# A first product by another set of seven block products, with partial results put into PSUM by ScalarE and VectorE

## The chip, the cores and the metric

The kernel runs on one core of a Trainium2 chip. The metric is the device time of one execution in microseconds (us). Times inside the kernel come from the hardware profile of one execution: TensorE is PE, its weight loads are PEld, VectorE is DVE, ScalarE is ACT, GpSimd is POOL and SyncE is SP.

## The reference

```python
batch, m, k, h, n = 16, 512, 768, 3072, 768
y = np.matmul(x, w1) + b1                    # x (16, 512, 768), w1 (768, 3072)
y = 0.5 * y * (1.0 + erf(y / np.sqrt(2.0)))  # GELU
return np.matmul(y, w2).astype(np.float32)   # w2 (3072, 768)
```

Two matrix products stand around a GELU. All inputs are float32 normal random numbers; the kernel multiplies in bf16 and sums in float32. The 16 x 512 = 8192 rows of x are independent of each other.

## The kernel before

**Pairs.** The 8192 rows are cut into pairs of row groups. A pair holds two halves of `w` rows each: w is 384 in pairs 0 to 9 and 256 in pair 10, the last. Both products are done in blocks, two by two, with seven block products in place of eight (Strassen's way): sums of blocks are multiplied, and sums of the seven results give the four blocks wanted. The first product of pair 0 and of the first `PLAIN = 3` positions of pair 1 is done plainly (`plain`), while the sums of w1 blocks are still being made (`make_w1`).

**First product.** H = 3072 is 24 chunks of 128, and K = 768 is 6 chunks. For a position j (0 to 11) the four results are the chunks j and 12 + j of H for the two halves of the rows: c11, c12, c21 and c22, in the code's order. Each of seven block products (M1 to M7) is three matmuls of 128 x 128 weights with a moving operand of w columns (`product1`, line 162). The weights are seven ready-made forms of w1 for that j, 672 KB, which SP loads from `w1f` in DRAM into a ring of seven slots of `w1t` (`load_slot`). The moving operands are blocks of x, transposed, in `xt` (written by DMA transposes that SP issues, `prepare_x`), and sums of such blocks in `xft`, made by VectorE (`sum_x`).

**PSUM banks.** There are eight banks in three pools: `ps_x` (3), `ps_y` (3) and `ps_z` (2). M4, M5 and M7 are summed in one bank (X), M3, M2 and M6 in another (Y), and M1 has the third (Z), see `BANK`. After each product one engine reads the bank (`evacuate`): ScalarE copies M4 into `x1` and M1 into `z` (line 99), VectorE makes `q` (line 106) and subtracts four times into `tt` (line 109). ScalarE then takes the GELU of two results at a time, from `tt` into `g` (lines 170 and 174, 128 x 768).

**Order of the first product.** Every engine runs its instructions in the order of the program (`inorder`). The steps overlap by hand:

```python
for d, m in ((2, "M7"), (1, "M5"), (0, "M4"), (2, "M6"), (1, "M2"), (0, "M3"), (0, "M1")):
    step1(s - d, m)
```

so the products of one j are spread over three steps. M6, the last user of a slot, issues the reload of that slot for seven positions on.

**Second product.** It uses the same seven products over 12 positions j, for each sub-block of 128 rows (three in a wide pair, two in the last): `part2` (line 205, 12 matmuls of 384 columns for each M), `gsum` for the sums of `g` into `st`, `finish2` for the read-out and the output DMA. M4 and M3 use `g` itself and begin early, between the last products of the first product (`early`). At the end of a pair, while `rest(2, ...)` runs, VectorE makes the input sums of the next pair (`xsums`), and the last group of the pair is `rest(2, "M6")`.

**The last pair.** With w = 256 a first-product matmul streams 256 columns; the second product's matmuls keep 384, since their moving operand is a half of w2.

Of the kernel before, what the change touches and what calls it, by code (L numbers as in the profile page):

```python
# [8 lines left out]
FP32 = mybir.dt.float32  # L9
# [3 lines left out]
P = 128  # L13
# [8 lines left out]


WF = {"M3": 0, "M4": 1, "M1": 2, "M5": 3, "M2": 4, "M6": 5, "M7": 6}
XF = {"M3": 0, "M4": 1, "M1": 2, "M6": 3, "M7": 4}
SF = {"M1": 0, "M5": 1, "M2": 2, "M7": 3, "M6": 4}
BANK = {"M1": "Z", "M3": "Y", "M2": "Y", "M6": "Y", "M4": "X", "M5": "X", "M7": "X"}

# [2 lines left out]
def kernel(  # L31
# [8 lines left out]
    nc = tc.nc  # L40
# [108 lines left out]
            dma(nc.sync, out=slot(idx), in_=w1f[(idx + PLAIN) % HP, :, :])  # L149

    def moving1(m, kc, w):
        if m == "M2":
            return xt[:, kc, 0, :w]
        if m == "M5":
            return xt[:, KH + kc, 1, :w]
        return xft[:, XF[m], kc, :w]

    def product1(t, m, p, j, w):
        ps = bank(t, m)
        forms = slot((p - 1) * HP + j - PLAIN).rearrange("p (f kc c) -> p f kc c", f=7, kc=KH)  # L160
        for kc in range(KH):
            inorder(nc.tensor.matmul(  # L162
                out=ps[:, :w], lhsT=forms[:, WF[m], kc, :], rhs=moving1(m, kc, w),
                start=(kc == 0 and m in ("M1", "M3", "M4")), stop=(kc == KH - 1),
                skip_group_check=True))
        tj = tt[:, j % 2]
        c = {"11": tj[:, 0, :w], "12": tj[:, 1, :w], "21": tj[:, 2, :w], "22": tj[:, 3, :w]}
        evacuate(t, m, w, c)
        if m == "M7":
            inorder(nc.scalar.activation(out=g[:, j, :, :w], in_=tj[:, 0:2, :w], func=ACTF.Gelu,  # L170
                                         bias=b1t[:, j:j + 1], scale=1.0))
        if m == "M6":
            load_slot((p - 1) * HP + j - PLAIN + RING)
            inorder(nc.scalar.activation(out=g[:, HP + j, :, :w], in_=tj[:, 2:4, :w], func=ACTF.Gelu,  # L174
                                         bias=b1t[:, HP + j:HP + j + 1], scale=1.0))


    def rows(h, half, i, j0=0, j1=HP):
# [59 lines left out]
            inorder(nc.sync.dma_start_transpose(out=xt[:, :, half, c0:c0 + P], in_=xb[:]))  # L238

    def sum_x(k, w):  # L240
        b11, b12 = xt[:, :KH, 0, :w], xt[:, :KH, 1, :w]
        b21, b22 = xt[:, KH:, 0, :w], xt[:, KH:, 1, :w]
        if k == 0:
            sub(xft[:, XF["M4"], :, :w], b11, b21)
        elif k == 1:
            sub(xft[:, XF["M3"], :, :w], b22, b12)
        elif k == 2:
            add(xft[:, XF["M1"], :, :w], b11, b22)
        elif k == 3:
            add(xft[:, XF["M7"], :, :w], b21, b22)  # L250
        else:
            add(xft[:, XF["M6"], :, :w], b11, b12)


    def load_w2(j, n):
# [33 lines left out]
    def make_w1():  # L289
        nonlocal made  # L290
        j = (made + PLAIN) % HP
        a = raw(j)
        if made < HP - PLAIN:
            area, o = ((ttb, 0), (ttb, 3072), (xftf, 0), (xftf, SLOT))[made % 4]
        else:
            area, o = ((stf, 0), (stf, SLOT), (ttb, 0))[made - HP + PLAIN]
        made += 1
        s = area[:, o:o + SLOT].rearrange("p (f kc c) -> p f kc c", f=7, kc=KH)
        copy("act", s[:, 0:2], a[:, 0:4:3])
        add(s[:, 2], a[:, 0], a[:, 3])  # L300
        add(s[:, 3:5], a[:, 0:4:2], a[:, 1:4:2])
        sub(s[:, 5], a[:, 0], a[:, 2])
        sub(s[:, 6], a[:, 3], a[:, 1])
        dma(nc.sync, out=w1f[j], in_=area[:, o:o + SLOT])

    def plain(hc, half):
# [95 lines left out]
    late_w2 = [lambda k=k, part=part: make_w2(k, part) for part in range(2) for k in range(9, HP)]  # L402


    for p, (r0, w) in enumerate(pairs):
        ns = w // P
        subs = [dict() for _ in range(ns)]
        most = HP - 2
        nxt = pairs[p + 1] if p + 1 < len(pairs) else None

        def early(i, m, a, b):
            part2(subs[i], m, i, a, b)

        def both(i, a, b, close):
            for m in ("M4", "M3"):
                early(i, m, a, b)
                if close:
                    finish2(subs[i], m, r0, w, i)

        def rest(i, m, after=()):  # L420
            part2(subs[i], m, i, 0, HP)
            finish2(subs[i], m, r0, w, i)
            for f in after:
                f()

        def sums(i, *ms):
            return [lambda m=m: gsum(m, i) for m in ms] if i < ns else []

        def xsums(*ks):
            return [lambda k=k: sum_x(k, nxt[1]) for k in ks] if nxt is not None else []  # L430

        forms = [make_w1] if p == 0 else []

        if p == 0:
            for m in ("M1", "M5", "M2"):
                gsum(m, 0)
                late_w2.pop(0)()
            for f in late_w2:
                f()
            for m in ("M7", "M6"):  # L440
                gsum(m, 0)
            for j in range(HP - 1):
                for i in range(ns):
                    early(i, "M3", j, j + 1)
                for i in range(ns):
                    early(i, "M4", j, j + 1)
            both(0, HP - 1, HP, True)
            both(1, HP - 1, HP, True)
        else:
            js = list(range(PLAIN if p == 1 else 0, HP))  # L450
            if p == 1:
                while made < HP:
                    make_w1()
                for j in range(PLAIN):
                    for hc in (j, HP + j):
                        plain(hc, 0)
                        plain(hc, 1)
                load_raw_slots(PLAIN)
                for k in range(5):
                    sum_x(k, w)  # L460
            ts = [dict() for _ in range(HP)]

            def step1(s, m):
                if 0 <= s < len(js):
                    product1(ts[s], m, p, js[s], w)

            for s in range(len(js)):
                for d, m in ((2, "M7"), (1, "M5"), (0, "M4"), (2, "M6"), (1, "M2"), (0, "M3"), (0, "M1")):
                    step1(s - d, m)
            last = len(js) - 1  # L470
            step1(last - 1, "M7")
            step1(last, "M5")
            early(0, "M4", 0, 5)
            step1(last - 1, "M6")
            step1(last, "M2")
            gsum("M1", 0, 0, most)
            early(0, "M4", 5, most)
            early(0, "M3", 0, most)
            step1(last, "M7")
            step1(last, "M6")  # L480
            gsum("M5", 0, 0, most)
            early(1, "M4", 0, most)
            early(1, "M3", 0, most)
            both(0, most, HP, True)
            gsum("M1", 0, most, HP)
            gsum("M5", 0, most, HP)
            for m in ("M2", "M7", "M6"):
                gsum(m, 0)

        if nxt is not None:  # L490
            prepare_x(*nxt)
        nload = 0

        def load_raw_slots(plain_done=0):
            nonlocal nload
            while nload < RING:
                k = (nload + FIRST) % RING
                need = {j for j in range(HP)
                        if j // 3 * 2 * GRP < (k + 1) * SLOT and (j // 3 + 1) * 2 * GRP > k * SLOT}
                have = {(PLAIN + n) % HP for n in range(made)}  # L500
                if not need <= have or any(plain_done <= j < PLAIN for j in need):
                    break
                load_slot(nload)
                nload += 1

        def forms(n):
            if p > 0:
                return []

            def f():  # L510
                make_w1()
                load_raw_slots()
            return [f] * n

        rest(0, "M1")
        rest(0, "M5", sums(1, "M1"))
        rest(0, "M2", sums(1, "M5"))
        if p == 0:
            both(2, HP - 1, HP, True)
        rest(0, "M7", sums(1, "M2") + forms(1))  # L520
        rest(0, "M6", sums(1, "M7", "M6"))
        if p > 0:
            both(1, most, HP, True)
        rest(1, "M1", forms(1))
        rest(1, "M5", sums(2, "M1") + forms(1))
        rest(1, "M2", sums(2, "M5"))
        rest(1, "M7", sums(2, "M2"))
        rest(1, "M6", sums(2, "M7", "M6"))
        if ns > 2:
            if p > 0:  # L530
                both(2, 0, HP, True)
            later = p == 0
            rest(2, "M1", forms(1) if later else xsums(0, 1))
            rest(2, "M5", forms(1) if later else xsums(2))
            rest(2, "M2", forms(1) if later else xsums(3))
            rest(2, "M7", () if later else xsums(4))
            rest(2, "M6")


# [28 lines left out]
```

## Time and profile before

| what | value |
|---|---|
| runs | 900.15, 900.21 and 901.23 us, median 900.21 |
| span of the profiled execution | 897.6 us |
| its own device time | not listed apart; the median is 2.6 us over the span |
| PE busy | 889.9 us, 5627 matmuls |
| DVE busy | 597.1 us, 1088 instructions |
| ACT busy | 380.4 us, 609 instructions |
| mean granted TensorE clock | 1.000 |
| first product, line 162 | 2457 matmuls, from 111.9 to 869.4 us |

In timeline rows the columns are the start in us, the time the row covers, the engine, the line of the kernel, the operation, what it writes and reads, the shape and the number of instructions merged; in brackets stands how long the engine had been idle, and what released it. In rows of groups, behind the bar stand the busy time in us and the mean duration of one in ns, then the idle time before them. In rows of waits stand the total in us, the number of times and the longest. The recorded duration of a matmul covers its way through the array, so successive matmuls overlap in the record, and their starts tell the rate.

### The profile page before, as it was taken

The numbers are of one execution on the slowest core, as the hardware profiler recorded it, in microseconds if no ns is written. First come the engines' busy times: TensorE is split into PE (matmuls) and PEld (weight loads), VectorE is DVE, ScalarE is ACT, GpSimd is POOL, SyncE is SP. The second block draws the span as 40 slices with busy tenths as digits, with TensorE's granted clock in tenths as the row PEclk, the third lists the DMA queues.
The fourth block names the chain that finished last, engine by engine and source line by source line (L and its number), as shares of the span: only waits on it lengthen the run. The fifth ranks groups of instructions, "written<-read, shape, count | busy, mean of one in ns | idle before, by whom it ended". The sixth has DMA issues, their size and how long they took to land.

```text
span 897.6 us, 14279 instructions
## 1 busy us (share of the span) xinstructions
PE 889.9 (99%) x5627; PEld 544.2 (61%) x5627; DVE 597.1 (67%) x1088; ACT 380.4 (42%) x609; POOL 81.3 (9%) x148
## 2 busy tenths in 40 slices
PE   8999999999999999999999999999999999999998
PEld 5656666666666666666666666666666666666774
DVE  1287776677667676766776676767667766766665
ACT  3542474057217603730571175037306711750460
POOL 6200100100110010001001100100010011001000
PEclk9999999999999999999999999999999999999999
DMA  9997976556736663665557366746645663663411
GB/s 170 206 230 201 377 258 163 122 154 207 162 95 200 197 144 100 205 167 115 175 192 165 94 194 203 141 112 197 167 106 178 205 155 98 194 194 106 146 45 71
DMA packets 89159, 148.30 MB, mean 165 GB/s; under 512 B 50796, under 2 KB 68228, under 8 KB 89092
## 3 DMA queue, kind: packets, MB, share of 16 engines
q1 hardware_dynamic: 65588, 101.77, 37.6%
q0 software_dynamic: 23504, 45.62, 23.0%
q8 instruction: 44, 0.72, 0.3%
q14 instruction: 23, 0.19, 0.1%
HBM read 124.56 MB, written 33.42 MB: 176 GB/s over the span
## 4 chain that ended last, share of the span: by engine, by line
PE 98%; DMA 1%; POOL 0%; issue 0%; ACT 0%; DVE 0%; POOLq 0%
PE psx L205 21%; PE psy L205 21%; PE psx L162 18%; PE psy L162 18%; PE psz L205 7%; PE psz L162 6%; PE psy L312 3%; PE psx L312 3%; DMA st<-in_x_dram 1%; PE psy L375 0%; PE psx L375 0%; PE psz L341 0%; POOL st L74 0%; POOL w1t L74 0%; ACT g L314 0%
## 5 line engine op out<-in xcount | busy, mean ns | idle before, releaser
L162 PEld LDWEIGHTS <-w1t 128*128 128x128 bf16 x2457 | 240.0, 98 | 146.1
L205 PEld LDWEIGHTS <-st 128*128 128x128 bf16 x1920 | 187.6, 98 | 124.4
L99 ACT COPY x<-psx 128x384 f32<-128x384 f32 (+1 forms) x149 | 68.0, 457 | 266.8 <-PE psx L205 191.0
L162 PE MATMUL psx<-xft,w1t 128*128 128x384 bf16 (+1 forms) x702 | 148.6, 321 | 0.0
L162 PE MATMUL psy<-xft,w1t 128*128 128x384 bf16 (+1 forms) x702 | 148.5, 321 | 0.0
L170 ACT ACTIVATE g<-tt,b1t 128x768 bf16<-128x768 f32 (+1 forms) x117 | 106.9, 914 | 86.6 <-DVE tt L109 86.6
L205 PE MATMUL psx<-w2t,st 128*128 128x384 bf16 x768 | 135.3, 326 | 0.0
L205 PE MATMUL psy<-w2t,st 128*128 128x384 bf16 x768 | 135.3, 326 | 0.0
L106 DVE TENSOR_TENSOR q<-x,psy 128x384 f32<-128x384 f32 (+1 forms) x149 | 80.9, 543 | 55.6 <-ACT x L99 40.5
L174 ACT ACTIVATE g<-tt,b1t 128x768 bf16<-128x768 f32 (+1 forms) x117 | 106.7, 912 | 22.6 <-DVE tt L109 22.6
L99 ACT COPY z<-psz 128x384 f32<-128x384 f32 (+1 forms) x149 | 69.8, 468 | 93.6 <-PE psz L205 71.5
L205 PEld LDWEIGHTS <-g 128*128 128x128 bf16 x768 | 75.0, 98 | 50.0 <-issue 0.6
L109 DVE TENSOR_TENSOR tt<-z,psx 128x384 f32<-128x384 f32 (+1 forms) x117 | 63.3, 541 | 51.7 <-PE psx L162 51.7
L109 DVE TENSOR_TENSOR tt<-z,psy 128x384 f32<-128x384 f32 (+1 forms) x117 | 63.3, 541 | 45.9 <-PE psy L162 45.9
L106 DVE TENSOR_TENSOR st<-g 128x1536 bf16<-128x1536 bf16 (+2 forms) x116 | 92.5, 812 | 0.0
L74 POOL DMA_DIRECT2D xb<-in_x_dram x58 | 31.2, 542 | 523.9 <-DMA xt<-xb 515.5
L162 PE MATMUL psy<-xt,w1t 128*128 128x384 bf16 (+1 forms) x351 | 74.3, 321 | 0.0
L162 PE MATMUL psz<-xft,w1t 128*128 128x384 bf16 (+1 forms) x351 | 74.3, 321 | 0.0
L162 PE MATMUL psx<-xt,w1t 128*128 128x384 bf16 (+1 forms) x351 | 74.3, 321 | 0.0
L205 PE MATMUL psx<-w2t,g 128*128 128x384 bf16 x384 | 74.2, 326 | 0.0
L205 PE MATMUL psy<-w2t,g 128*128 128x384 bf16 x384 | 72.9, 326 | 0.3 <-ACT g L314 0.3
L205 PE MATMUL psz<-w2t,st 128*128 128x384 bf16 x384 | 67.7, 326 | 0.0
(53 smaller groups left out, 548.0 us busy)
## 6 DMA issues: line engine op xcount, KB each, us to landing
w1t<-w1f SPq DMA_DIRECT2D x117, 672.0 KB, 4.0
out_dram<-ot POOLq DMA_DIRECT2D x60, 384.0 KB, 2.6
xb<-in_x_dram POOLq DMA_DIRECT2D x58, 192.0 KB, 4.1
w2t<-in_w_dram POOLq DMA_DIRECT2D x8, 576.0 KB, 22.5
w1t<-in_w_dram POOLq DMA_DIRECT2D x7, 576.0 KB, 17.9
w1f<-tt SPq DMA_DIRECT2D x6, 672.0 KB, 4.8
w1f<-xft SPq DMA_DIRECT2D x4, 672.0 KB, 3.6
out_dram<-ot SPq DMA_DIRECT2D x4, 384.0 KB, 2.3
```

What stands on the lines that cost most here:

```text
L74: inorder(queue.dma_start(out=out, in_=in_))
L99: inorder(nc.scalar.copy(out=dst, in_=src))
L106: inorder(nc.vector.tensor_tensor(out=dst, in0=a, in1=b, op=ALU.add))
L109: inorder(nc.vector.tensor_tensor(out=dst, in0=a, in1=b, op=ALU.subtract))
L162: inorder(nc.tensor.matmul(out=ps[:, :w], lhsT=forms[:, WF[m], kc, :], rhs=moving1(m, kc, w), start=(kc == 0 and m in ("M1", "M3", "M4")), ...
L170: inorder(nc.scalar.activation(out=g[:, j, :, :w], in_=tj[:, 0:2, :w], func=ACTF.Gelu, bias=b1t[:, j:j + 1], scale=1.0))
L174: inorder(nc.scalar.activation(out=g[:, HP + j, :, :w], in_=tj[:, 2:4, :w], func=ACTF.Gelu, bias=b1t[:, HP + j:HP + j + 1], scale=1.0))
L205: inorder(nc.tensor.matmul(out=ps[:, :NB], lhsT=lhs, rhs=w2t[:, j, WF[m], :], start=(j == 0 and m in ("M1", "M3", "M4")), stop=(j == HP - ...
L312: inorder(nc.tensor.matmul(out=py[:, :HW], lhsT=lhs[:, kc, (j % 3) * P:(j % 3 + 1) * P], rhs=xt[:, kc, half, :], start=(kc == 0), stop=(kc ...
```

## The change

The first product uses another set of seven products, P1 to P7, and other block sums. They are gathered in three banks for each j:

- c12's bank (pool Z): P1 opens it and P4 adds to it. The GELU reads it from PSUM.
- c11's bank (pool X): ScalarE copies P1 from c12's bank into it, as a start value. P2, P6 and P3 add to it, none of them opening the bank. The GELU reads it from PSUM after P3.
- c22's bank (pool Y): P7 opens it, and VectorE copies it to SBUF (`v`). After P2 VectorE writes c11's bank minus `v` over it, and P5 adds to that. The GELU reads it from PSUM, with scale -1.
- c21 never has a bank: after P6 VectorE writes c11's bank minus `v` to `tt`, and the GELU reads it there, with scale -1.

So VectorE has three instructions for each j where it had five, and ScalarE has one copy and four GELUs of w columns, where it had two copies and two GELUs of 2 w. Four sums of x blocks are made where there were five; the fourth uses the third, which uses the second. The products of one j span two steps. The first two products of a pair, P1 and P7 of its first j, are issued ahead of the last group of the pair before (`ahead`), and in pair 1 ahead of the last plain half.

```diff
-XF = {"M3": 0, "M4": 1, "M1": 2, "M6": 3, "M7": 4}
+W1F = {"P7": 0, "P1": 1, "P2": 2, "P3": 3, "P4": 4, "P6": 5, "P5": 6}
+XF = {"P1": 0, "P3": 1, "P2": 2, "P7": 3}
+XRAW = {"P4": (1, 0), "P6": (0, 1), "P5": (1, 1)}
...
+    def gelu1(j, h, half, src, w, sign):
+        hc = h * HP + j
+        inorder(nc.scalar.activation(out=g[:, hc, half, :w], in_=src, func=ACTF.Gelu,
+                                     bias=b1t[:, hc:hc + 1], scale=sign))
+
     def product1(t, m, p, j, w):
-        ps = bank(t, m)
+        if m == "P1":
+            t["c12"] = ps_z.tile([P, 512], FP32, name="psz")
+            ps = t["c12"]
+        elif m == "P4":
+            ps = t["c12"]
+        elif m == "P7":
+            t["c22"] = ps_y.tile([P, 512], FP32, name="psy")
+            ps = t["c22"]
+        elif m == "P5":
+            ps = t["c22"]
+        else:
+            ps = t["c11"]
...
-                out=ps[:, :w], lhsT=forms[:, WF[m], kc, :], rhs=moving1(m, kc, w),
-                start=(kc == 0 and m in ("M1", "M3", "M4")), stop=(kc == KH - 1),
+                out=ps[:, :w], lhsT=forms[:, W1F[m], kc, :], rhs=moving1(m, kc, w),
+                start=(kc == 0 and m in ("P1", "P7")), stop=(kc == KH - 1),
...
+        if m == "P1":
+            t["c11"] = ps_x.tile([P, 512], FP32, name="psx")
+            copy("act", t["c11"][:, :w], ps)
+        elif m == "P7":
+            t["v"] = evp.tile([P, HW], FP32, name="z")
+            copy("dve", t["v"][:, :w], ps)
+        elif m == "P2":
+            sub(t["c22"][:, :w], ps, t["v"][:, :w])
+        elif m == "P6":
+            sub(tt[:, j % 2, 0, :w], ps, t["v"][:, :w])
+        elif m == "P4":
+            gelu1(j, 1, 0, ps, w, 1.0)
+        elif m == "P3":
             load_slot((p - 1) * HP + j - PLAIN + RING)
+            gelu1(j, 0, 0, ps, w, 1.0)
+        elif m == "P5":
+            gelu1(j, 0, 1, tt[:, j % 2, 0, :w], w, -1.0)
+            gelu1(j, 1, 1, ps, w, -1.0)
...
+        a11, a12 = xt[:, :KH, 0, :w], xt[:, KH:, 0, :w]
+        a21, a22 = xt[:, :KH, 1, :w], xt[:, KH:, 1, :w]
...
+            sub(f[:, XF["P1"]], a11, a12)
+            add(f[:, XF["P3"]], a11, a21)
+            sub(f[:, XF["P2"]], a12, f[:, XF["P3"]])
+            add(f[:, XF["P7"]], f[:, XF["P2"]], a22)
...
+    def ahead(p):
+        j = PLAIN if p == 1 else 0
+        for m in ("P1", "P7"):
+            product1(ts[p][j], m, p, j, pairs[p][1])
...
-                for d, m in ((2, "M7"), (1, "M5"), (0, "M4"), (2, "M6"), (1, "M2"), (0, "M3"), (0, "M1")):
+                if s == 0:
+                    order = ((0, "P2"), (0, "P4"), (-1, "P1"), (0, "P6"))
+                elif s == 1:
+                    order = ((0, "P7"), (1, "P5"), (0, "P2"), (1, "P3"), (0, "P4"), (0, "P6"))
+                else:
+                    order = ((0, "P1"), (0, "P7"), (1, "P5"), (0, "P2"), (1, "P3"), (0, "P4"), (0, "P6"))
+                for d, m in order:
                     step1(s - d, m)
...
-            step1(last - 1, "M7")
-            step1(last, "M5")
+            step1(last, "P5")
             early(0, "M4", 0, 5)
-            step1(last - 1, "M6")
-            step1(last, "M2")
+            step1(last, "P3")
             gsum("M1", 0, 0, most)
             early(0, "M4", 5, most)
             early(0, "M3", 0, most)
-            step1(last, "M7")
-            step1(last, "M6")
...
-            rest(2, "M7", () if later else xsums(4))
+            rest(2, "M7")
+            if nxt is not None and p > 0:
+                ahead(p + 1)
             rest(2, "M6")
```

More of the change, by code (lines that the diff above doesn't have):

```diff
@@ L151, in moving1 @@
     def moving1(m, kc, w):
[L152 to L155, printed above, removed]
+        if m in XRAW:
+            kh, half = XRAW[m]
+            return xt[:, kh * KH + kc, half, :w]
         return xft[:, XF[m], kc, :w]
+    def gelu1(j, h, half, src, w, sign):
+        hc = h * HP + j
+        inorder(nc.scalar.activation(out=g[:, hc, half, :w], in_=src, func=ACTF.Gelu,
+                                     bias=b1t[:, hc:hc + 1], scale=sign))
     def product1(t, m, p, j, w):
-        ps = bank(t, m)
+        if m == "P1":
[10 more added lines that the diff above has]
+            ps = t["c11"]
         forms = slot((p - 1) * HP + j - PLAIN).rearrange("p (f kc c) -> p f kc c", f=7, kc=KH)
@@ L162, in product1 @@
             inorder(nc.tensor.matmul(
-                out=ps[:, :w], lhsT=forms[:, WF[m], kc, :], rhs=moving1(m, kc, w),
-                start=(kc == 0 and m in ("M1", "M3", "M4")), stop=(kc == KH - 1),
+                out=ps[:, :w], lhsT=forms[:, W1F[m], kc, :], rhs=moving1(m, kc, w),
+                start=(kc == 0 and m in ("P1", "P7")), stop=(kc == KH - 1),
                 skip_group_check=True))
[L166 to L172, printed above, removed]
+        ps = ps[:, :w]
+        if m == "P1":
[11 more added lines that the diff above has]
+        elif m == "P3":
             load_slot((p - 1) * HP + j - PLAIN + RING)
-            inorder(nc.scalar.activation(out=g[:, HP + j, :, :w], in_=tj[:, 2:4, :w], func=ACTF.Gelu,
-                                         bias=b1t[:, HP + j:HP + j + 1], scale=1.0))
+            gelu1(j, 0, 0, ps, w, 1.0)
+        elif m == "P5":
+            gelu1(j, 0, 1, tt[:, j % 2, 0, :w], w, -1.0)
+            gelu1(j, 1, 1, ps, w, -1.0)
     def rows(h, half, i, j0=0, j1=HP):
@@ L240, in sum_x @@
     def sum_x(k, w):
-        b11, b12 = xt[:, :KH, 0, :w], xt[:, :KH, 1, :w]
-        b21, b22 = xt[:, KH:, 0, :w], xt[:, KH:, 1, :w]
+        a11, a12 = xt[:, :KH, 0, :w], xt[:, KH:, 0, :w]
+        a21, a22 = xt[:, :KH, 1, :w], xt[:, KH:, 1, :w]
+        f = xft[:, :, :, :w]
         if k == 0:
-            sub(xft[:, XF["M4"], :, :w], b11, b21)
+            sub(f[:, XF["P1"]], a11, a12)
         elif k == 1:
-            sub(xft[:, XF["M3"], :, :w], b22, b12)
+            add(f[:, XF["P3"]], a11, a21)
         elif k == 2:
-            add(xft[:, XF["M1"], :, :w], b11, b22)
-        elif k == 3:
-            add(xft[:, XF["M7"], :, :w], b21, b22)
+            sub(f[:, XF["P2"]], a12, f[:, XF["P3"]])
         else:
-            add(xft[:, XF["M6"], :, :w], b11, b12)
+            add(f[:, XF["P7"]], f[:, XF["P2"]], a22)
     def load_w2(j, n):
@@ L298, in make_w1 @@
         s = area[:, o:o + SLOT].rearrange("p (f kc c) -> p f kc c", f=7, kc=KH)
-        copy("act", s[:, 0:2], a[:, 0:4:3])
-        add(s[:, 2], a[:, 0], a[:, 3])
+        copy("act", s[:, 0:2], a[:, 1:3])
+        add(s[:, 2], a[:, 1], a[:, 2])
         add(s[:, 3:5], a[:, 0:4:2], a[:, 1:4:2])
-        sub(s[:, 5], a[:, 0], a[:, 2])
-        sub(s[:, 6], a[:, 3], a[:, 1])
+        sub(s[:, 5], a[:, 2], a[:, 0])
+        sub(s[:, 6], a[:, 1], a[:, 3])
         dma(nc.sync, out=w1f[j], in_=area[:, o:o + SLOT])
@@ L402 @@
     late_w2 = [lambda k=k, part=part: make_w2(k, part) for part in range(2) for k in range(9, HP)]
+    ts = [[dict() for _ in range(HP)] for _ in pairs]
+    def ahead(p):
+        j = PLAIN if p == 1 else 0
+        for m in ("P1", "P7"):
+            product1(ts[p][j], m, p, j, pairs[p][1])
     for p, (r0, w) in enumerate(pairs):
@@ L450 @@
             js = list(range(PLAIN if p == 1 else 0, HP))
+            last = len(js) - 1
             if p == 1:
@@ L453 @@
                     make_w1()
[L454 to L457, printed above, removed]
+                for k in range(4):
+                    sum_x(k, w)
+                hcs = [hc for j in range(PLAIN) for hc in (j, HP + j)]
+                for hc in hcs:
+                    plain(hc, 0)
+                    if hc == hcs[-1]:
+                        ahead(p)
+                    plain(hc, 1)
                 load_raw_slots(PLAIN)
-                for k in range(5):
-                    sum_x(k, w)
-            ts = [dict() for _ in range(HP)]
             def step1(s, m):
-                if 0 <= s < len(js):
-                    product1(ts[s], m, p, js[s], w)
-            for s in range(len(js)):
-                for d, m in ((2, "M7"), (1, "M5"), (0, "M4"), (2, "M6"), (1, "M2"), (0, "M3"), (0, "M1")):
+                if 0 <= s <= last:
+                    product1(ts[p][js[s]], m, p, js[s], w)
+            for s in range(last + 1):
+                if s == 0:
[5 more added lines that the diff above has]
+                for d, m in order:
                     step1(s - d, m)
-            last = len(js) - 1
-            step1(last - 1, "M7")
-            step1(last, "M5")
+            step1(last, "P5")
             early(0, "M4", 0, 5)
-            step1(last - 1, "M6")
-            step1(last, "M2")
+            step1(last, "P3")
             gsum("M1", 0, 0, most)
```

## The prediction

> **What bounds the kernel now.** I read the page first, then who waited for whom, then the timeline of one step of the first product, once in a wide pair (moving width 384) and once in the last pair (width 256), and last the groups with shapes kept apart.
>
> The page says that TensorE is never without work, at full clock:
>
> ```profile
> span 897.6 us, 14279 instructions
> PE 889.9 (99%) x5627; PEld 544.2 (61%) x5627; DVE 597.1 (67%) x1088; ACT 380.4 (42%) x609; POOL 81.3 (9%) x148
> PEclk9999999999999999999999999999999999999999
> ```
>
> Busy time alone proves little, because the ends of matmuls are modelled. The timeline settles it. These rows are one step of the first product in a wide pair:
>
> ```profile
> 207.97 0.65 PE L162 MATMUL psx<-xft,w1t 128*128 128x384 bf16 x3
> 208.45 0.65 PE L162 MATMUL psx<-xt,w1t 128*128 128x384 bf16 x3
> 208.65 0.56 DVE L109 TENSOR_TENSOR tt<-z,psx 128x384 f32<-128x384 f32 x1 [0.35 <-PE psx L162]
> ...
> 211.38 0.65 PE L162 MATMUL psx<-xft,w1t 128*128 128x384 bf16 x3
> ```
>
> From M7 of one step (207.97) to M7 of the next (211.38) are 3.41 us for 21 matmuls, 0.1625 us each. Twelve matmuls of the second product of the same width take 1.95 us in the chain of waits, again 0.1625 each. In the last pair a step takes 845.99 - 843.70 = 2.29 us, 0.109 us a matmul:
>
> ```profile
> 843.70 0.49 PE L162 MATMUL psx<-xft,w1t 128*128 128x256 bf16 x3
> ...
> 844.23 0.42 DVE L109 TENSOR_TENSOR tt<-z,psx 128x256 f32<-128x256 f32 x1 [0.16 <-PE psx L162]
> ...
> 845.99 0.49 PE L162 MATMUL psx<-xft,w1t 128*128 128x256 bf16 x3
> ```
>
> So rate and count of the matmuls set the time, and in the list of waits TensorE is held by another compute engine once after the start:
>
> ```profile
> PE psy L205 <- ACT g L314: 0.3, 1, 0.3
> ```
>
> That wait lies at 59 us, in pair 0, which the change leaves alone. The first product has nothing to win back; it can only lose.
>
> **The change, part by part.**
>
> *Matmuls.* Seven products of three matmuls before, seven of three after, same widths: 2205 of 384 columns and 252 of 256. Cost 0.
>
> *Work of VectorE and ScalarE.* Per j VectorE loses five additions or subtractions (0.555 us each) and gains one copy and two subtractions. ScalarE trades two copies and two wide GELUs for one copy (0.47) and four GELUs of 384 (the row L314 has 0.58, and they start 0.46 apart when queued, as at 104.72 and 105.18): 0.47 + 4 x 0.46 = 2.3 us of each 3.41. Neither engine bounds anything; relieving them is worth nothing while TensorE has the chain.
>
> *The new waits of TensorE.* Before, every read-out had most of a step before its bank or result was wanted. Now two read-outs stand between products of the same step. The order is P1 P7 P5' P2 P3' P4 P6 (a prime marks the step before).
>
> First wait: P2 waits for ScalarE's copy of P1 into the bank c11. P2 is due three products after P1 begins, 9 x 0.1625 = 1.463 us. A read-out begins 0.69 us after its product begins (207.97 to 208.65, rounded). An instruction whose TensorE wait stands in a wait of its own ahead of it begins about 0.07 later: in the last pair M7's subtraction normally begins 0.53 after M7 (843.70, 844.23), and where it has such a double wait 0.60 after (868.89, 869.49):
>
> ```profile
> 868.89 0.49 PE L162 MATMUL psx<-xft,w1t 128*128 128x256 bf16 x3
> ...
> 869.49 0.42 DVE L109 TENSOR_TENSOR tt<-z,psx 128x256 f32<-128x256 f32 x1 [1.61 <-PE psx L162]
> ```
>
> The new copy has a double wait too; ScalarE's rows of that kind come 0.06 late (a copy at 873.38 begins 0.42 after its last matmul, others 0.36). The copy takes 0.47. From its end to the matmul I take 0.05, from the one stall that the trace shows (58.98 + 0.58 = 59.56, matmul at 59.61):
>
> ```profile
> 58.98 0.58 ACT L314 ACTIVATE g<-psy,b1t 128x384 bf16<-128x384 f32 x1 [0.17 <-PE psy L312]
> 59.61 0.32 PE L205 MATMUL psy<-w2t,g 128*128 128x384 bf16 x1 [0.34 <-ACT g L314]
> ```
>
> Sum: 0.69 + 0.06 + 0.47 + 0.05 = 1.27 of 1.46: hidden with 0.19 to spare. ScalarE must be free then: its last GELU before it (P4' of the step before) begins at five products plus 0.69 = 3.13 and lets go at 3.59, against 3.41 + 0.75 = 4.16. Behind the waiting copy stand the four GELUs, which nobody on TensorE wants within the step.
>
> Second wait: P6 waits until VectorE has read c11 (`sub(t["c22"]...)`, PSUM to PSUM). P6 too is due 9 matmuls after P2 begins. Sum: 0.69 + 0.07 + 0.555 + 0.05 = 1.365 of 1.463: hidden with 0.10 to spare. VectorE is free: its copy of P7 ends by 0.27 after P2 begins. Behind the subtraction waits only P6's own.
>
> In the last pair the same two sums have nine matmuls of 0.1092 = 0.983 us. ScalarE: 0.53 + 0.06 + 0.355 + 0.05 = 0.995, late by 0.01. VectorE: 0.60 + 0.42 + 0.05 = 1.07, late by 0.09. Durations are from
>
> ```profile
> L109 DVE TENSOR_TENSOR tt<-psx,q 128x256 f32<-128x256 f32 x12 | 5.0, 418 | 0.2 <-PE psx L162 0.2
> L99 ACT COPY x<-psx 128x256 f32<-128x256 f32 x12 | 4.3, 355 | 7.9 <-PE psx L162 7.9
> ```
>
> Twelve steps: 12 x 0.09 + 11 x 0.01 = 1.2 us, all on the path.
>
> *The unknown price* is a VectorE or ScalarE write to PSUM; every such row of before writes SBUF. The tail behind an instruction's last read is what could differ: VectorE starts its next 0.46 after one of 0.555 (89.01 to 89.47), a tail of 0.095. With no tail nothing is late anywhere: 0 us, and below nothing it can't go, since TensorE has no idle time there to give. With a tail twice as long the wide pairs still just fit (0.69 + 0.07 + 0.65 + 0.05 = 1.46) and the last pair is late by 0.18 x 12 = 2.2 us. I take the SBUF duration, the nearest row: on the reading side the space makes no difference (fp32 from PSUM: 558 ns for 384 columns and 424 for 256, so 1.05 a column and 156 fixed; bf16 from SBUF: 948 for 1536 and 352 for 384, 0.52 a column and 153 fixed).
>
> The Trainium skill (Perfetto Trace Analysis, section Optimizing Scalar/DVE Operations) gives about 60 ns of access overhead for VectorE on SBUF and 125 on PSUM, and 93 and 51 for ScalarE. On reads the rows here do not agree; on writes no run so far shows it. By it the last pair would be late by 0.155 instead of 0.09 a step, +1.9 us in all.
>
> *Edits at nothing.* The ring reload (`load_slot`) is issued by P3, one step behind, instead of M6, two behind: six products, 2.9 us, earlier on SP; its loads land in 4.0 us, seven steps ahead, and no TensorE wait names them; the x transposes stand behind it as before. P1 and P7 ahead of the second product's last group: P7 needs the fourth input sum, which VectorE makes right after M2's read-out, about 0.36 + 0.56 + 0.75 = 1.7 us after M2's last matmul begins, against 12 + 3 matmuls = 2.4. In pair 1 the five sums end at 108.2 us, and P1 would begin one plain half before 111.93, at 110.95. If one of these covers went, it would cost under 1 us per pair, 10 us in all. One bank of c11, c12 and c22 is reused after 3, 2 and 3 steps, longer than the read-outs take.
>
> **The rivals.**
>
> *VectorE's write to PSUM is longer than 0.655 us in wide pairs (slower).* From there on P6 is late in all 117 steps. At 0.70: 105 x 0.045 + 12 x 0.23 = 7.5 us, 907.7. Between 0.605 and 0.655 only the last pair pays, 1.8 to 2.4 us, 902.0 to 902.6. For it: 0.10 is a thin cover, and no row has this write. Against: VectorE's rows move by less than 10 ns with the source. Chance 0.27 for both together. (The Trainium skill, same section, says that profiled latency is about twice its figures; its difference counted twice makes 0.685 and, as an estimate, 906.)
>
> *No stall at all.* The PSUM write is acknowledged faster, and the last pair just fits: 900.2. Chance 0.08.
>
> *ScalarE becomes late.* Its queue is strict; were the copy delayed by a GELU by more than 0.19, each of 117 steps would pay the rest. Per 0.05 that is 5.9 us, 906. Against: 0.57 us between its last GELU and the copy. Chance 0.06.
>
> *The clock falls.* Should the short stalls of the last pair halve the clock there, its 27.5 us of first product double: about 928. Against: the granted clock is 1.000 in every slice past a 0.5 us stall at 59 us. The Trainium skill (TensorE: Matmul & The Clock Gate, section A second HAM failure mode: psum-queue depth-cycling) reports such a case. Chance 0.03.
>
> *Faster.* It would need time that TensorE loses now; that is some 7 us at the start, which no edit touches, and the 0.3. Chance 0.03, for what I have overlooked.
>
> **How the numbers follow.** The profiled span is 897.6 and the median of the runs 900.21; the 2.6 around the span stay. The forecast is 900.21 + 1.2 = 901.4, with a chance of 0.53 that it ends within 900.4 to 902.0. A measurement of this kernel can tell some 0.2%, 1.8 us, from no change: so forecast and "no stall" count as the same (0.61), the write, ScalarE and the clock as slower (0.36), the rest as faster (0.03). The range runs from 899.9 (no stall, with the runs' scatter) to 904.0, which takes in both ends of the unknown write and the milder half of the slow rival.
>
> **What would show it.** Right: in wide pairs first-product matmuls still 0.1625 apart, P6 without idle time before it; in the last pair about 0.09 before each P6. Wrong: P6 waiting in all pairs (VectorE's write over 0.655), P2 waiting for ScalarE's copy, or TensorE waiting for sums or slots at a pair's start. A time below 898.4 would contradict the bound itself.

## The result and the profile after

| kernel | runs, us | ratio to before, 95% interval |
|---|---|---|
| before | 899.78 to 901.39, median 900.64 (6) | |
| changed | 901.76 to 904.30, median 903.03 (6) | 1.0033, 1.0019 to 1.0047 |

The changed kernel is slower, by 2.4 us in this comparison. It was forecast at 901.4, within 899.9 to 904.0: the median lies in that range, but outside the narrower 900.4 to 902.0, to which the prediction gave a chance of 0.53. A second comparison further down gives 1.0009 (0.9998 to 1.0019), and there the change's part is told from the start's.

The page of after, against that of before: the same matmuls, a fifth less VectorE time (479.8 us in place of 597.1), a span 2.4 us longer, and the granted clock of TensorE full in every slice.

```profile
span 900.0 us, 14009 instructions
PE 890.6 (99%) x5627; PEld 544.6 (61%) x5627; DVE 479.8 (53%) x844; ACT 371.1 (41%) x726; POOL 81.4 (9%) x148
```

VectorE lost 117 us of work and ScalarE 9, and none of it came out as time, since the first product's matmuls had not waited for either before.

A wide step, from the timeline:

```profile
202.71 0.65 PE L179 MATMUL psx<-xft,w1t 128*128 128x384 bf16 x3
202.97 0.57 DVE L111 TENSOR_TENSOR psy<-psx,z 128x384 f32<-128x384 f32 x1 [0.47 <-PE psx L179]
203.20 0.65 PE L179 MATMUL psz<-xt,w1t 128*128 128x384 bf16 x3
203.69 0.65 PE L179 MATMUL psx<-xt,w1t 128*128 128x384 bf16 x3
204.17 0.65 PE L179 MATMUL psz<-xft,w1t 128*128 128x384 bf16 x3
204.66 0.65 PE L179 MATMUL psy<-xft,w1t 128*128 128x384 bf16 x3
204.92 0.46 ACT L101 COPY psx<-psz 128x384 f32<-128x384 f32 x1 [0.45 <-PE psz L179]
205.15 0.65 PE L179 MATMUL psy<-xt,w1t 128*128 128x384 bf16 x3
205.63 1.14 PE L179 MATMUL psx<-xft,w1t 128*128 128x384 bf16 x6
```

The rows are P3', P4, P6, P1, P7, P5' and P2 with P3' again. They begin 0.49 us apart, without a gap: VectorE's subtraction ends at 202.97 + 0.567 = 203.54 and P6 is due at 203.69; ScalarE's copy ends at 205.38 and P2 is due at 205.63.

The same in the last pair:

```profile
850.52 0.43 DVE L111 TENSOR_TENSOR psy<-psx,z 128x256 f32<-128x256 f32 x1 [0.29 <-PE psx L179]
850.59 0.49 PE L179 MATMUL psz<-xt,w1t 128*128 128x256 bf16 x3
851.01 0.49 PE L179 MATMUL psx<-xt,w1t 128*128 128x256 bf16 x3
```

From P4 (850.59) to P6 (851.01) are 0.42 us where three matmuls take 0.33: a wait of 0.09. The subtraction ends at 850.957, P6 begins at 851.01. By the starts of all matmuls, P6 waits 0.09 nine times, 0.03 twice and 0.17 once in the last pair, 1.04 us together.

Two more waits of 0.25 us lie in wide pairs, at 128 and 609 us. The first:

```profile
127.87 0.65 PE L179 MATMUL psz<-xt,w1t 128*128 128x384 bf16 x3
128.00 0.57 DVE L111 TENSOR_TENSOR psy<-psx,z 128x384 f32<-128x384 f32 x1 [0.83 <-ACT g L161]
128.61 0.65 PE L179 MATMUL psx<-xt,w1t 128*128 128x384 bf16 x3
```

Here VectorE's subtraction for P6 began 0.13 after P4, where in the usual step it begins 0.23 ahead of P4 (202.97 against 203.20): 0.36 late, which is more than the cover of 0.10. The ScalarE instruction named in brackets had ended at 127.67.

All waits of the first product add up to 1.54 us, by the starts of successive matmuls less 0.1625 or 0.1092 each; the same sum over before is 0.00. The other 0.8 us of the longer span lies at the start, which the change leaves alone: the first matmuls that need w1 begin at 9.38 in the profile of before and at 10.10 here, both after a wait for the load, and 0.1 more goes into the wait for the next load of w1.

```profile
9.38 1.18 PE L375 MATMUL psx<-xt,w1t 128*128 128x128 bf16 x18 [1.84 <-DMA w1t<-in_w_dram]
```

```profile
10.10 1.18 PE L400 MATMUL psx<-xt,w1t 128*128 128x128 bf16 x18 [3.21 <-DMA w1t<-in_w_dram]
```

### The profile page after: what moved, and what is told of

Its sections match the earlier page's. It is cut to its first block, busy times and chain, and to the rows that moved or that the text cites. A ratio compares the mean times of both kernels' runs of the same rounds, so it can differ in the third digit from the quotient of the medians.

```text
span 900.0 us, 14009 instructions
## 1 busy us (share of the span) xinstructions
PE 890.6 (99%) x5627; PEld 544.6 (61%) x5627; DVE 479.8 (53%) x844; ACT 371.1 (41%) x726; POOL 81.4 (9%) x148
## 4 chain that ended last, share of the span: by engine, by line
PE 98%; DMA 1%; ACT 0%; POOL 0%; issue 0%; DVE 0%; ACTq 0%; POOLq 0%
PE psx L231 21%; PE psy L231 21%; PE psx L179 18%; PE psz L179 12%; PE psy L179 12%; PE psz L231 7%; PE psy L337 3%; PE psx L337 3%; DMA st<-in_x_dram 1%; PE psy L400 0%; ACT g L161 0%; PE psx L400 0%; PE psz L366 0%; DVE psy L111 0%; POOL st L76 0%
## 5 line engine op out<-in xcount | busy, mean ns | idle before, releaser
L179 PE MATMUL psx<-xft,w1t 128*128 128x384 bf16 (+1 forms) x702 | 131.0, 320 | 0.0
L111 DVE TENSOR_TENSOR tt<-psx,z 128x384 f32<-128x384 f32 (+1 forms) x117 | 63.6, 544 | 103.0 <-PE psx L179 103.0
L101 ACT COPY psx<-psz 128x384 f32<-128x384 f32 (+1 forms) x117 | 53.0, 453 | 94.4 <-PE psz L179 94.4
L111 DVE TENSOR_TENSOR psy<-psx,z 128x384 f32<-128x384 f32 (+1 forms) x117 | 64.7, 553 | 49.3 <-PE psx L179 47.6
L103 DVE COPY z<-psy 128x384 f32<-128x384 f32 (+1 forms) x117 | 63.7, 544 | 39.3 <-PE psy L179 39.2
L161 ACT ACTIVATE g<-psx,b1t 128x384 bf16<-128x384 f32 (+1 forms) x117 | 66.6, 569 | 38.5 <-PE psx L179 37.0
L161 ACT ACTIVATE g<-psz,b1t 128x384 bf16<-128x384 f32 (+1 forms) x117 | 66.5, 569 | 26.6 <-PE psz L179 26.6
L161 ACT ACTIVATE g<-tt,b1t 128x384 bf16<-128x384 f32 (+1 forms) x117 | 70.9, 606 | 11.5 <-DVE tt L111 11.5
L179 PE MATMUL psz<-xt,w1t 128*128 128x384 bf16 (+1 forms) x351 | 74.2, 321 | 0.0
L179 PE MATMUL psy<-xft,w1t 128*128 128x384 bf16 (+1 forms) x351 | 74.2, 321 | 0.0
```

The costliest lines, as they stand in the source:

```text
L101: inorder(nc.scalar.copy(out=dst, in_=src))
L103: inorder(nc.vector.tensor_copy(out=dst, in_=src))
L111: inorder(nc.vector.tensor_tensor(out=dst, in0=a, in1=b, op=ALU.subtract))
L161: inorder(nc.scalar.activation(out=g[:, hc, half, :w], in_=src, func=ACTF.Gelu, bias=b1t[:, hc:hc + 1], scale=sign))
L179: inorder(nc.tensor.matmul(out=ps[:, :w], lhsT=forms[:, W1F[m], kc, :], rhs=moving1(m, kc, w), start=(kc == 0 and m in ("P1", "P7")), stop ...
```

## The experiments

**Theory A:** the change costs what its two new waits cost, 1.5 us in the first product; the rest is scatter of the start. **Theory B:** it also lowers the clock, or the loss lies elsewhere.

**1. Before against itself, and the change again.** No edit.

> The kernel before against itself. Theory A (the change costs what TensorE waits for in the first product, 1.5 us in the trace, and the rest of the measured 2.4 us is scatter of the start): ratio 1.000, and the granted clock of the single executions scatters as it does for the changed kernel (0.996 to 1.000). Theory B (the change also lowers the clock in most executions): all executions of this kernel at a clock of 1.000, while the changed kernel has 0.996 to 0.998.

> The changed kernel once more, on the chip of the other runs of this set. Theory A: 1.5 us over before, ratio 1.0017, with 0.09 us of waiting ahead of nine or ten P6 of the last pair and one or two longer waits elsewhere. Theory B: 2.4 us or more, ratio 1.0027 to 1.004, with a clock below that of before.

Measured: before against itself 0.9998 (0.9989 to 1.0007), 901.4 against 901.48 for the 29 executions of before in this set; the change 902.67, ratio 1.0009 (0.9998 to 1.0019). Both kernels have executions at mean clocks from 0.996 to 1.000, so theory B's clock is refuted. Sorted by that clock (means, with the number of executions; the changed kernel has none at 0.997), the difference is much the same in each group, though some groups are small and the times within one differ by up to 2 us:

| mean clock | before against itself | the 29 of before | changed | changed less the 29 |
|---|---|---|---|---|
| 0.996 | 902.07 (1) | 902.32 (11) | 903.48 (1) | 1.16 |
| 0.998 | 901.37 (4) | 901.43 (9) | 902.79 (8) | 1.36 |
| 1.000 | 899.75 (2) | 899.95 (5) | 901.02 (3) | 1.07 |

The trace of the second run of the change has 1.51 us of waits in the first product (1.54 in the first run), ahead of the same instructions. So the change's own cost is 1.1 to 1.4 us by the times and 1.5 by the trace, and of the 2.4 in the first comparison about one is scatter. The scatter's place is in the trace of this run: after the wait for w1 its clock falls for some microseconds.

```profile
8.00:12.00 4.00, 2.07 (x22) 2.08 (x23) 0.00 (x0) 0.00 (x0) 1.67 (x2) 0.78 1.15 199
12.00:16.00 4.00, 3.99 (x59) 3.83 (x57) 1.11 (x2) 1.54 (x3) 3.17 (x4) 0.80 1.27 202
```

These are rows of busy time by stretch; the third number from the end is the granted clock, 1.00 in both stretches in the profiles of before. Here 0.22 and 0.20 of 4 us are missing, 1.7 us at full clock, about as much as lies between the executions of before at 1.000 and at 0.998 (1.5).

**2. P6 later.**

```diff
-    order = ((0, "P1"), (0, "P7"), (1, "P5"), (0, "P2"), (1, "P3"), (0, "P4"), (0, "P6"))
+    order = ((0, "P1"), (1, "P6"), (0, "P7"), (1, "P5"), (0, "P2"), (1, "P3"), (0, "P4"))
```

with the first two steps and the end of a pair to match; there two groups of the second product's early matmuls move too. Between P1 and P2 lie three products then, P6', P7 and P5', not the four that the expectation names.

> P6 of a step is put behind P1 of the next, so that three products instead of two lie between P2 and P6, and four between P1 and P2; nothing else changes. Theory A (P6 waits for VectorE's subtraction into PSUM): P6 is then due 12 x 0.109 = 1.31 us after P2 in the last pair, against a need of 1.07, and 1.95 against 1.36 in the wide pairs, so no matmul of the first product waits: 1.5 us less than the changed kernel, ratio to before 1.000. Theory B (the loss is the clock's or lies outside the first product): the waits go from the trace, but the time stays 1 us or more over before.

Measured: 901.42, ratio 1.0000 (0.9991 to 1.0009). The sum of waits in the first product is 0.00 us again. In the last pair:

```profile
849.01 0.43 DVE L111 TENSOR_TENSOR psy<-psx,z 128x256 f32<-128x256 f32 x1 [0.21 <-ACT g L161]
849.08 0.49 PE L179 MATMUL psz<-xt,w1t 128*128 128x256 bf16 x3
849.41 0.49 PE L179 MATMUL psz<-xft,w1t 128*128 128x256 bf16 x3
849.73 0.49 PE L179 MATMUL psx<-xt,w1t 128*128 128x256 bf16 x3
```

P4, the next P1 and P6 follow each other at 0.33 us; the subtraction ends at 849.44, 0.29 before P6. Theory A holds, and this order takes the change's whole cost away. It does not beat the kernel before: neither has a gap in TensorE's first product.

**3. One product between P2 and P6 instead of two.**

```diff
-    order = ((0, "P1"), (0, "P7"), (1, "P5"), (0, "P2"), (1, "P3"), (0, "P4"), (0, "P6"))
+    order = ((0, "P1"), (0, "P7"), (1, "P5"), (0, "P4"), (0, "P2"), (1, "P3"), (0, "P6"))
```

> From the third step of a pair on, P4 is issued ahead of P2, so that only one product (P3 of the step before) lies between P2 and P6. The sum of the read-out chain (0.69 + 0.06 + 0.57 + 0.05 = 1.37 us wide, 0.59 + 0.43 + 0.05 = 1.07 in the last pair) against six matmuls (0.975 and 0.655) gives a wait of 0.39 us ahead of P6 in 87 wide steps and 0.42 in 10 narrow ones: 34 + 4 us, some 37 us over the changed kernel, near 939. If the chain were not what holds P6 (a rival: the bank is free as soon as VectorE has read its last element, some 0.1 us before the subtraction's recorded end), the wait would be 0.29, and the time near 929.

Measured: 939.57, ratio 1.0424 (1.0398 to 1.0451). By the starts P6 waits 0.388 us in a usual wide step; all waits make 38.0 us, 36.5 over the changed kernel. So the recorded end of the subtraction counts, not an earlier release of the bank, with which P6 would have waited 0.29.

```profile
202.38 0.57 DVE L111 TENSOR_TENSOR psy<-psx,z 128x384 f32<-128x384 f32 x1 [0.96 <-PE psx L179]
203.00 0.65 PE L179 MATMUL psx<-xt,w1t 128*128 128x384 bf16 x3 [0.22 <-DVE psy L111]
```

The row of P6 shows idle time of only 0.22, since the recorded ends of the matmuls ahead are modelled and reach into the wait. The list of waits has the same shortfall:

```profile
PE psx L179 <- DVE psy L111: 22.2, 97, 0.6
```

22 us in place of 38. In the changed kernel, where the waits are 0.03 to 0.25, the list names no such wait at all.

**4. One product between P1 and P2.**

```diff
-    order = ((0, "P1"), (0, "P7"), (1, "P5"), (0, "P2"), (1, "P3"), (0, "P4"), (0, "P6"))
+    order = ((0, "P1"), (0, "P7"), (0, "P2"), (1, "P5"), (1, "P3"), (0, "P4"), (0, "P6"))
```

> From the third step of a pair on, P2 is issued ahead of P5 of the step before: only P7 lies between P1 and P2, and three products between P2 and P6. Theory A (the copy of P1 by ScalarE is a chain of 0.69 + 0.06 + 0.47 + 0.05 = 1.27 us wide and 0.53 + 0.06 + 0.36 + 0.05 = 1.00 in the last pair): P2 is due after six matmuls, 0.975 and 0.655, so it waits 0.29 us in 87 wide steps and 0.34 in 10 narrow ones, 25 + 3.4 us, less the 0.9 that P6 no longer waits in the last pair: some 28 us over the changed kernel, near 930. Rival (ScalarE writes PSUM with a much shorter tail, so that its cover was larger than it seemed): clearly less than 0.25 a step.

Measured: 928.65, ratio 1.0311 (1.0289 to 1.0333). P2 waits 0.28 us in a usual wide step and 0.23 in the third step of a pair; all waits make 27.2 us, 25.7 over the changed kernel. Some 28 were expected; the third steps wait less than was taken, and the two waits of 0.25 in wide pairs went as well, since P6 now has a product more of room. ScalarE's chain is as long as its rows say.

**5. P1 and P7 not ahead.**

```diff
-                    if hc == hcs[-1]:
-                        ahead(p)
...
-                if s == 0:
-                    order = ((0, "P2"), (0, "P4"), (-1, "P1"), (0, "P6"))
+                if s == 0:
+                    order = ((0, "P1"), (0, "P7"), (0, "P2"), (0, "P4"), (-1, "P1"), (0, "P6"))
...
-            if nxt is not None and p > 0:
-                ahead(p + 1)
```

> P1 and P7 of a pair's first j are issued at the pair's start, not ahead of the last group (in pair 1: not ahead of the last plain half). Theory A: at each start only P7 lies between P1 and P2, so P2 waits 0.29 us for ScalarE's copy in nine wide pairs and 0.34 in the last, 3.0 us over the changed kernel, ratio to before near 1.0045. Rival (the order at the start of a pair costs nothing, since matmuls are queued deep): the same as the changed kernel.

Measured: 904.93, ratio 1.0043 (1.0028 to 1.0057). The waits make 3.48 us, 1.9 over the changed kernel, less than the 3.0 expected: 0.23 us instead of 0.29 in eight pairs, 0.28 in pair 1 and in the last; the last pair's first P6 waits 0.03 in place of 0.17, and of the two waits of 0.25 in wide pairs only the first is left. At a pair's start the copy carries no double wait:

```profile
186.14 0.65 PE L179 MATMUL psz<-xft,w1t 128*128 128x384 bf16 x3
186.83 0.46 ACT L101 COPY psx<-psz 128x384 f32<-128x384 f32 x1 [7.81 <-PE psz L179]
187.35 0.65 PE L179 MATMUL psx<-xft,w1t 128*128 128x384 bf16 x3
```

It begins 0.69 after P1, not 0.75. The rival, that the order at a pair's start is free, is refuted.

**6. Three more VectorE instructions.**

```diff
+    for _ in range(3):
+        inorder(nc.vector.memset(tt[:, 0, 0, 0:2], 0.0))
```

> The changed kernel with three more tiny VectorE instructions at the start, nothing else. Theory A (the two waits of 0.25 us ahead of P6 in wide pairs come from the place of the subtraction in VectorE's instruction stream: in the changed kernel it is instruction 193 and 833 of the engine, both one past a multiple of 64 and 640 apart, and an 8 KB instruction transfer of 128 instructions of 64 bytes lies beside the second): the waits go from the 5th and 74th subtraction (near 128 and 609 us) to the 20th and 105th, which now stand at such places (near 218 and 795 us); the time stays. Rival (they come from what other transfers do at that time): they stay near 128 and 609 us or come and go.

Measured: one execution, 902.76, too few to judge the time by. The waits at 128 and 609 us are gone, and two of 0.25 us stand at 221 and 798 us, ahead of the P6 of the 20th and the 105th subtraction:

```profile
221.01 0.65 PE L179 MATMUL psz<-xt,w1t 128*128 128x384 bf16 x3
221.13 0.57 DVE L111 TENSOR_TENSOR psy<-psx,z 128x384 f32<-128x384 f32 x1 [0.82 <-ACT g L161]
221.75 0.48 PE L179 MATMUL psx<-xt,w1t 128*128 128x384 bf16 x2
```

So these two waits hang on the place of an instruction in VectorE's stream. The places themselves stayed late: the instructions that now stand where the two subtractions stood, P6's subtractions into `tt` at 127.07 and 608.47, begin 0.36 and 0.35 us later than usual as well, and nothing on TensorE wants them soon. Counted in the trace, waits included, the two places are 192 and 832 (193 and 833 in the expectation's count); VectorE's instructions that are 0.35 or 0.36 us late in the other traces stand multiples of 128 from these two. The place alone is not enough: in the first run of the change the subtraction at place 704 comes on time, at 513.94, where VectorE was still busy with the instruction ahead.

What happens at these places stays open. An 8 KB instruction transfer is recorded within a microsecond of each of the two in the changed kernel, but the nearest begins after the late subtraction has begun (128.68 after 128.00, 609.48 after 609.41), so the subtraction did not wait for that one to land.

## Why the prediction was right, and where it was not

*The bound.* TensorE's rate and the number of matmuls set the time; the first product had nothing to win. Shown by experiment 2: with every wait in the first product removed the time is that of before, 1.0000, though VectorE has a fifth less to do.

*The first wait, 1.27 us against 1.46.* Measured: the copy takes 0.464 into PSUM (0.47 taken), begins 0.75 after P1 and leaves 0.20 of cover (0.19 said). Experiment 4 turns the cover into a wait of 0.28 (0.29).

*The second wait, 1.365 us against 1.463.* Measured: the subtraction takes 0.567 (0.555 taken), the step from its end to the matmul 0.053 (0.05), the double wait 0.057 (0.07). That these small errors cancel is luck; the cover is 0.10 as said. Experiment 3 gives 0.388 (0.39).

*The last pair, 1.2 us.* Measured 1.04 ahead of P6. VectorE's part was right, 0.09 a step in nine steps; in two the double wait was missing, and in the first the read-out of the second product's last group (0.555 long) stood ahead of the subtraction on VectorE, so that P6 waited 0.17. The forecast had checked VectorE's queue only within the usual step. ScalarE's 0.01 a step is there too: in nine steps P2 begins 0.05 after the copy's end and 0.008 later than the rate gives. In the sum of 1.54 these 0.07 us are made up again, since the matmuls behind a wait follow about 0.001 closer than 0.1092.

*The unknown price.* A write to PSUM costs VectorE 0.01 us more than one to SBUF, in rows side by side:

```profile
L111 DVE TENSOR_TENSOR psy<-psx,z 128x384 f32<-128x384 f32 x105 | 59.5, 567 | 46.2 <-PE psx L179 44.5 <-ACT g L161 1.7
L111 DVE TENSOR_TENSOR tt<-psx,z 128x384 f32<-128x384 f32 x105 | 58.5, 557 | 95.3 <-PE psx L179 95.3
```

The slower rival needed 0.655 or more. The difference of 65 ns that the Trainium skill gives for VectorE (Perfetto Trace Analysis, section Optimizing Scalar/DVE Operations) is not seen here, neither in reads (a fixed 156 ns from PSUM, 153 from SBUF, in the rows of before) nor in writes (567 and 557).

*The clock.* No stall of the first product touched it. In experiment 3 P6 waits 0.33 to 0.42 us in 95 steps and 0.74 in two; these waits sum to 38.0 us, the time is 38.1 over before, and the granted clock is 1.00 all through the first product. So the Trainium skill's case (TensorE: Matmul & The Clock Gate, section A second HAM failure mode: psum-queue depth-cycling) is not this one. In the first product the clock falls in no trace; it falls after the wait of some microseconds at the start, and not in every execution. Executions of before have the same mean clocks, down to 0.996, but neither of its two traces holds such a fall.

*What failed.* The step "edits at nothing" missed the place of VectorE's instructions in their stream, 0.5 us; that the last pair cost 0.2 less than forecast hides a part of it. And the step from the sum to the median took the scatter of the start too lightly: the first comparison has 2.4 us over before where 1.2 was forecast, while the trace has 1.54. The scatter was already in the 2.6 us between span and median, which the prediction lets stay: every later execution takes about 1.8 longer than its span, so the profiled execution of before was 0.8 quicker than the median. The first comparison passed the 0.2% line within which the text had called a result the same; the sum itself (1.2) and the change's own cost (1.1 to 1.5) lie on its near side. The way to look for waits, "P6 without idle time before it", was also poor: idle time hides waits of this size (0.22 shown for 0.388 in experiment 3), starts show them.

## What to carry to other kernels

When one engine is fed without a gap, as here, taking work from the others is worth nothing, and every result that now has to come back within the step has a deadline: count the matmuls between producer and user, and set against them the read-out chain (start delay, duration, way back), for the narrowest shape first: from 384 to 256 columns P6's deadline shrank by 0.48 us and the chain by 0.30. Give each such chain room for one late instruction (0.36 us here); one product more between P2 and P6 removed the whole cost. To find waits shorter than a matmul's recorded length, read the starts of successive matmuls, not the idle time.

## What the runs showed that was not expected

An instruction of VectorE can come 0.36 us late by its place in the instruction stream: subtractions at the same two places were late in both runs of the changed kernel and in experiments 3 and 4, and three instructions put ahead made others late that then stood at such places. What delays them is not known.

The start decides much of the scatter. The wait for the first w1 load was between 1.84 and 3.21 us in the profiles shown, and in some executions the clock then stays low for several microseconds: 18 matmuls of 128 columns that take 1.18 us in the profile of before take 1.87 in the second run of the change.
